# Column groups of a projection taken in pairs, seven products of halves instead of eight

## The chip, the cores and the metric

The kernel runs on one core of one Trainium2 chip. The metric is the device time of one execution in microseconds (us); lower is better. A core has TensorE (matrix products into PSUM), VectorE, ScalarE and GpSimd (element-wise work; GpSimd reads no PSUM here), and SyncE, whose queue starts most DMAs. In the profile's rows they are PE (PEld for its weight loads), DVE, ACT, POOL and SP.

## The reference

Two layers of a hybrid block on `x` of 512 rows by 1024 columns, all float32. In each layer:

```
h = rmsnorm(x, norm_g)
u = h @ w_in                      # 1024 x 9312; columns split into named parts
ml:  q, k by a causal convolution of 4 taps and silu; mLSTM over 4 heads of 256 with gates i, f
     y_ml  = rmsnorm(mlstm * sigmoid(o)) * silu(z)
gla: gated linear attention, 4 heads (64 / 128), decay from a rank-16 projection
     y_gla = rmsnorm(gla) * silu(r)
dsa: scores of 8 small index heads choose 128 keys a query (top-k); attention over these, 4 heads
     y_dsa = dsa * silu(z)
x = x + concat(y_ml, y_gla, y_dsa) @ w_out     # 2048 x 1024
```

The projection `h @ w_in` and the product with `w_out` are most of the arithmetic.

## The kernel before

**Matmuls.** Each float32 operand is cut into a high and a low float32r part, and a product is three matmuls, high by high, high by low and low by high (`mm3`, line 509). `xhi` and `xlo` (405, 406) hold the two parts of the normed input, transposed: 8 blocks of 128 along the 1024 inputs (KT) by 512 rows.

**Column groups.** The columns of `w_in` are worked off in groups of 256, in the order of `group_order` (66): values of the GLA, a small group `misc`, index queries, GLA queries and keys, then PLAN (105): three ML heads (o, q, k, v), a closing, the fourth head, a closing, two DSA units, two closings. In the plain form (`proj_n`, 524; PSUM tile `pn`) the input is the stationary operand and 256 columns of weights are streamed: 4 row blocks by 8 k-blocks by 3 matmuls, 96 a group. In the transposed form (`proj_t`, 514; PSUM tile `pt`) the weights are stationary and the 512 rows are streamed: 2 column blocks by 8 by 3, 48 a group. A closing (`y_group`, 724, and `w_out_part`, 733) projects two gate groups, multiplies them into a branch's output (`y_part`, 693), and multiplies 512 columns of the result with their part of `w_out` in 8 chunks (PSUM tile `pw`), each added into the residual `xr`, which stays in SBUF (385).

**Weights.** They come from DRAM in halves of a group, 128x1024, on SP's queue (`load`, 449). ScalarE writes the high part, VectorE the low part (`split_part`, 467), a few halves ahead of use.

**Order.** The schedule is written out when the program is built. Between the matmuls of a group, `tick` (505) issues a part of the weight splitting and then stages of background tasks: recurrences, convolutions, attention, top-k. Whether a task's next stage is issued is read from a clock kept with estimated durations (`Clock`, 207; `Background.due`, 304): not before what it reads should be there, and not while ScalarE, VectorE or GpSimd would be more than 11 us behind. On the chip each engine takes its instructions in that fixed order and waits on semaphores. At the start of a layer the norm of a row block (`norm_in`, 625) squares, scales, transposes and splits it.

**PSUM.** Three banks rotate among projections (`pp`, 360), five among the background tasks (`pa`, 365).

Of the kernel before, what the change touches and what calls it, by code (L numbers as in the profile page):

```python
# [20 lines left out]
S = 512  # L21
D = 1024
# [42 lines left out]

def group_order():
    order = []

    def cols(name, g=0):
        order.append(("in", OFF[name] + 256 * g))  # L70

    def out(q):
        order.append(("out", 512 * q, 0))
        order.append(("out", 512 * q, 512))

    def unit(kind, g):
        if kind == "dsa":
            for n in ("dsa_q", "dsa_k", "dsa_v"):
                cols(n, g)
        else:  # L80
            for n in ML_ORDER:
                cols(n, g)

    def steps(plan):
        for step in plan:
            if step[0] == "close":
                for g in range(2):
                    cols(step[1], step[2] + g)
                out(step[3])
            else:  # L90
                unit(*step)

    cols("gla_v", 0)
    cols("gla_v", 1)
    order.append(("misc",))
    cols("idx_q", 0)
    cols("idx_q", 1)
    order.append(("gqk", 0))
    order.append(("gqk", 1))
    steps(PLAN)  # L100
    return order


ML_ORDER = ("ml_o", "ml_q", "ml_k", "ml_v")
PLAN = (("ml", 0), ("ml", 1), ("ml", 2), ("close", "ml_z", 0, 0), ("ml", 3), ("close", "gla_r", 0, 2), ("dsa", 0), ("dsa", 1), ("close", "ml_z", 2, 1), ("close", "dsa_z", 0, 3))


def pack_weights(w_in, w_out):
    order = group_order()
# [28 lines left out]
BEHIND = {"sel": ("dve",)}  # L138
BACKLOG = {None: 11.0, "sel": 0.3}
ALONE = ("gla", "ml", "sel", "scores")  # L140
BUFFERS = {"gla": 6, "dsa": 2, "ml": 4, "mlv": 1, "conv": 2, "qk": 2, "y": 2, "scores": 4, "gates": 5}
# [24 lines left out]
class Meter:  # L166
    """Passes instructions on to an engine and books them on the engine's estimated clock (us)."""
# [15 lines left out]
    def cost(self, op, args, kw):  # L183
# [3 lines left out]
        if self.name == "pe":  # L187
            if op == "transpose":
                return 0.109
            n, one_pass = free_size(out), kw["rhs"].dtype == F32R  # L190
            if one_pass:
                return max(n, 256) / 2400 + 0.002
            if out.shape[0] == 64:
                return max(n / 950, 0.08)
            return max(4 * n, 256) / 2400 + 0.004
# [11 lines left out]
class Clock:  # L207
    """Estimated time at which each engine gets done with what it has been given; an operation starts when
    its engine is free and what it reads has been written."""
# [12 lines left out]
    def ring(self, tag, tile, bufs):  # L222
        """The tile takes the place of the one made bufs tiles before it."""
        ring = self.rings.setdefault(tag, [])
        ring.append(tile.name)
        if len(ring) > bufs:
            old = ring.pop(0)
# [38 lines left out]
class Background:  # L266
    """Tasks cut into stages: a stage is issued once what the stage before it made should be there."""
# [36 lines left out]
    def due(self, task):  # L304
        late = BACKLOG.get(task["kind"], BACKLOG[None])
        return max(task["ready"], max(self.clock.at[e] for e in BEHIND.get(task["kind"], ("act", "dve", "pool"))) - late)
# [26 lines left out]
def hybrid_kernel(ctx, tc, a, out, dbg=None):  # L333
# [15 lines left out]
    N_T4, N_T2, N_F8, VA_BUFS = 9, 19, 2, 1  # L349
    W_BUFS, LOAD = 5, 4.5  # L350
# [19 lines left out]
    def t4(name, n=1024):  # L370
        return wk.tile([128, 1024], F32, tag="t4", name=name, bufs=N_T4)[:, 0:n]
# [3 lines left out]

    def f8(name):
        return wk.tile([128, 2048], F32R, tag="f8", name=name, bufs=N_F8)
# [7 lines left out]
    xr = const.tile([128, NB, D], F32, name="xr")  # L385

    def load_x(sb):
        nc.sync.dma_start(xr[:, sb, :], a["x"][0, 128 * sb:128 * sb + 128, :])

    load_x(0)  # L390
# [15 lines left out]
    xlo = const.tile([128, KT, S], F32R, name="xlo")  # L406
    qzs = [const.tile([128, 2, 64 * NB], F32, name=f"qz{i}") for i in range(2)]
# [5 lines left out]
    # (scale * mean + scale * eps) ** -0.5  # L413
# [4 lines left out]
    # two float32r parts of a value in PSUM, with a gain per partition and block: high first, low a stage later  # L418
# [23 lines left out]
    # one tag holds what was loaded and the low parts; a slot of it stays free while halves wait to be split  # L442
    order = [(layer, i) + spec for layer in range(DEPTH) for i, spec in enumerate(group_order())]
    halves_of = [1 if spec[2] == "misc" else 2 for spec in order]
    to_load = [(k, half) for k in range(len(order)) for half in range(halves_of[k])]
    loaded, ready, parts, half_done = {}, {}, [], []
    state = {"held": 0, "split": 0, "used": 0, "done": 0}

    def load(limit):
        while to_load and state["held"] < limit:  # L450
            state["held"] += 1
            k, half = to_load.pop(0)
            layer, i = order[k][:2]
            raw = wp.tile([128, 1024], F32, tag="w", name=f"raw{k}_{half}", bufs=W_BUFS)
# [3 lines left out]
    def split():  # L458
        k = state["split"]
        if k == len(order):  # L460
            return
# [43 lines left out]
    def tick():  # L505
        split_part()
        bg.tick()
# [848 lines left out]
```

## Time and profile before

| | |
|---|---|
| time, median of 3 runs | 1238.54 us (1236.86 to 1240.45) |
| profiled execution: its span, first to last instruction | 1236.4 us |
| what lies between that span and the median | 2.1 us |
| TensorE busy | 1215.7 us, 8308 matmuls |
| VectorE, ScalarE, GpSimd busy | 830.5, 583.2, 162.0 us |
| granted TensorE clock | 9 tenths or more in every slice |
| DMA | 107.98 MB, mean 87 GB/s |

The page gives no total for the profiled execution beyond its span; the span is its own time here, and the median of the runs stands beside it. Busy TensorE time is the union of matmuls whose ends are modelled, so that consecutive ones overlap in the rows; the distance between two starts is what one takes. Idle time of an engine that nothing waits for costs nothing.

### The profile page before, as it was taken

To read this page: it belongs to the slowest core of one execution; us is meant where nothing else is said; L and a number is where in the kernel's file an instruction comes from. 1 tells how busy PE (TensorE), PEld (TensorE's weight loads), DVE (VectorE), ACT (ScalarE), POOL (GpSimd) and SP (SyncE) were. 2 spreads that over 40 slices of the span, in tenths; PEclk is the share of its full clock that TensorE was granted. 3 is DMA by queue.
4 is the path that set the end of the run, shared out by engine and by line. 5 is a ranking of instruction groups with operands and counts; after the bars stand their busy time and mean duration, and the time that the engine had idled before them with its cause. 6 is when DMAs were issued, how large, how long until landed. Compare 5 with 4: busy or idle time off the path is not lost.

```text
span 1236.4 us, 20867 instructions
## 1 busy us (share of the span) xinstructions
PE 1215.7 (98%) x8308; PEld 1095.3 (89%) x8308; DVE 830.5 (67%) x1618; ACT 583.2 (47%) x1214; POOL 162.0 (13%) x293
## 2 busy tenths in 40 slices
PE   6999999999999999999999999999999999999998
PEld 6978889899889898998898889898988998989997
DVE  5479869796887844364556978888888875234643
ACT  6564546444153265542357544564442443554321
POOL 2003112300000013200010121031210000122000
PEclk9999999999999999999999999999999999999999
DMA  4333222222222223323223223122222322313222
GB/s 160 107 108 100 87 69 78 69 78 69 83 97 96 76 71 109 112 69 102 69 70 120 69 71 106 57 93 77 69 67 71 111 69 92 123 52 116 67 83 102
DMA packets 35169, 107.98 MB, mean 87 GB/s; under 512 B 5028, under 2 KB 8388, under 8 KB 35072
## 3 DMA queue, kind: packets, MB, share of 16 engines
q1 hardware_dynamic: 33136, 104.89, 26.0%
q8 instruction: 65, 1.06, 0.4%
q0 software_dynamic: 1200, 1.36, 0.3%
q10 hardware_dynamic: 736, 0.41, 0.1%
q14 instruction: 32, 0.26, 0.1%
HBM read 104.48 MB, written 3.43 MB: 87 GB/s over the span
## 4 chain that ended last, share of the span: by engine, by line
PE 93%; DVE 2%; ACT 2%; DMA 1%; POOL 1%; issue 1%; SPq 0%; DVEq 0%; POOLq 0%
PE pn L180 42%; PE pt L180 22%; PE pw L180 14%; PE psS L180 2%; PE pom L180 2%; PE pod L180 2%; PE psga L180 1%; PE pss L180 1%; PE pog L180 1%; PE psy L180 1%; DMA bs<-skew 1%; POOL bs L180 1%; PE psl L180 1%; DVE lo L180 1%; ACT xhi L180 1%
## 5 line engine op out<-in xcount | busy, mean ns | idle before, releaser
L180 PE MATMUL pn<-hi,xhi 128*128 128x256 f32 x1536 | 445.2, 290 | 0.0
L180 PE MATMUL pn<-hi,xlo 128*128 128x256 f32 x1536 | 434.4, 283 | 1.0 <-DVE xlo L180 1.0
L180 PE MATMUL pn<-lo,xhi 128*128 128x256 f32 x1536 | 433.6, 282 | 1.3 <-DVE lo L180 1.3
L180 DVE TENSOR_TENSOR lo<-raw,hi 128x1024 fp32r<-128x1024 f32 x178 | 221.9, 1247 | 184.4 <-ACT hi L180 178.1
L180 PEld LDWEIGHTS pn<-lo,xhi 128*128 128x128 f32 x1536 | 291.6, 190 | 4.0 <-DVE lo L180 1.7
L180 PEld LDWEIGHTS pn<-hi,xhi 128*128 128x128 f32 x1536 | 289.9, 189 | 4.4 <-PE psl L180 1.0
L180 PEld LDWEIGHTS pn<-hi,xlo 128*128 128x128 f32 x1536 | 290.3, 189 | 1.5 <-DVE xlo L180 1.5
L180 ACT ACTIVATE hi<-raw 128x1024 fp32r<-128x1024 f32 x178 | 188.1, 1057 | 117.2 <-DMA raw<-w_pack 89.4
L180 PE MATMUL pt<-xhi,hi 128*128 128x512 f32 (+1 forms) x400 | 158.8, 397 | 0.0
L180 PE MATMUL pt<-xlo,hi 128*128 128x512 f32 (+1 forms) x400 | 154.5, 386 | 0.0
L180 PE MATMUL pt<-xhi,lo 128*128 128x512 f32 (+1 forms) x400 | 154.5, 386 | 0.0
L180 PE MATMUL pw<-hi,yhi 128*128 128x512 f32 x256 | 102.2, 399 | 0.0
L180 PE MATMUL pw<-hi,ylo 128*128 128x512 f32 x256 | 101.6, 397 | 0.0
L180 PE MATMUL pw<-lo,yhi 128*128 128x512 f32 x256 | 101.4, 396 | 0.0
L180 PEld LDWEIGHTS pt<-xhi,hi 128*128 128x128 f32 x400 | 75.2, 188 | 17.6 <-issue 4.2
L180 PEld LDWEIGHTS pt<-xhi,lo 128*128 128x128 f32 x400 | 75.3, 188 | 15.3
L180 PEld LDWEIGHTS pt<-xlo,hi 128*128 128x128 f32 x400 | 75.4, 189 | 12.6
L180 DVE TENSOR_TENSOR xr<-pw,xr 128x512 f32<-128x512 f32 x64 | 44.1, 689 | 51.0 <-PE pw L180 50.9
L180 DVE SCALAR_TENSOR_TENSOR cacc<-cbuf,pv,cacc 128x512 f32<-128x512 f32 x96 | 74.5, 776 | 2.5 <-ACT cacc L180 0.2
L180 ACT ACTIVATE th<-pn 128x512 f32<-128x512 f32 x32 | 19.2, 599 | 86.7 <-PE pn L180 86.7
L180 PEld LDWEIGHTS pw<-hi,ylo 128*128 128x128 f32 x256 | 48.2, 188 | 12.6 <-DVE ylo L180 1.2
L180 ACT ACTIVATE cbuf<-pt 128x512 f32<-128x512 f32 x32 | 19.1, 597 | 84.0 <-PE pt L180 79.7
(187 smaller groups left out, 1694.9 us busy)
## 6 DMA issues: line engine op xcount, KB each, us to landing
raw<-w_pack SPq DMA_DIRECT2D x178, 512.0 KB, 3.9
xr<-x SPq DMA_DIRECT2D x4, 512.0 KB, 7.7
negm<-negm SPq DMA_DIRECT2D x8, 256.0 KB, 5.2
bs<-skew SPq DMA_DIRECT2D x8, 256.0 KB, 6.1
out_dram<-xr SPq DMA_DIRECT2D x8, 256.0 KB, 2.0
bs<-skew SPq DMA_DIRECT2D x8, 192.0 KB, 6.3
skew<-flat POOLq DMA_DIRECT2D x1, 1280.0 KB, 17.9
bs<-skew SPq DMA_DIRECT2D x8, 128.0 KB, 5.5
```

The costliest lines, as they stand in the source:

```text
L180: return f(*args, **kw)
```

## The change

Two column groups are projected together. The 512 rows of the input, the 1024 inputs and the two groups are each halved, so that the product is a 2 x 2 by 2 x 2 product of blocks: eight products of 256 rows by 512 inputs by 256 columns. It is computed as seven (Strassen, in Winograd's arrangement), of sums of input quadrants and sums of weight halves. Three of the sums of the input (`xsum`) are formed once a layer and split again in two parts; a fourth takes the place of the quadrant (rows 256 to 511, inputs 0 to 511) in `xhi` and `xlo` once the groups that use it plainly are done. The weight sums are formed on GpSimd for each pair, four additions of 128x1024. In each layer 15 pairs go this way: two for each ML head (q with k in the transposed form, o with v), three for DSA (q with k, v with v, q with k), four at the closings. The GLA values, `misc`, index queries, and GLA queries and keys stay as they were, and so does `w_out`.

Beside it: high parts, low parts, loaded halves and sums share one tag of 15 buffers; low parts go to GpSimd or VectorE, whichever the clock has free first; all large tiles share one tag of 12; the residual lives in DRAM, to which the closings but the last of a layer add with accumulating DMAs of GpSimd's queue, and the last one reads it back; chunks of `w_out` run over the row blocks in the order 2, 3, 0, 1; the transposed form streams 256 rows at a time; the DMA scratch is 2048 bytes and the copy of the bias goes in two halves.

```diff
-    N_T4, N_T2, N_F8, VA_BUFS = 9, 19, 2, 1
-    W_BUFS, LOAD = 5, 4.5
+    N_T4, N_T2 = 12, 16
+    W_BUFS, LOAD = 15, 4.5
...
-    xr = const.tile([128, NB, D], F32, name="xr")
+    resid = dram.tile([S, D], F32, name="resid", bufs=1)
...
+    xsum = [[const.tile([128, 4, 256], F32R, name=f"x{n}{part}") for part in "hl"] for n in "567"]
...
+                b11, b12, b22, b21 = (Raw((layer, at + g, half)) for g, half in ((0, 0), (1, 0), (1, 1), (0, 1)))
+                s1 = Raw(sources=(b11, b12))
...
+                s2 = Raw(sources=(s1, b22))
+                s4 = Raw(sources=(s2, b21))
+                room += [b11, b12, s1, b22, ("add", b12, b22), s2, b21, s4]
+                pieces_of.append([Piece(b11, n, -1.0)] + [Piece(r, n) for r in (b12, s2, b21, s1, s4, b22)])
...
+            nc.gpsimd.tensor_tensor(dst.tile, ins[0].tile, ins[1].tile, op=OP.add)
...
+            engine = nc.gpsimd if clock.at["pool"] + POOL_LOW < clock.at["dve"] else nc.vector
+            engine.tensor_tensor(lo, p.raw.tile, hi.bitcast(F32), op=OP.subtract)
...
+    def prepare():
+        make_room()
+        said = [add_up(), split_low(), split_high()]
+        return said
...
     def tick():
-        split_part()
+        prepare()
         bg.tick()
...
+    def pair(form, f, dest=lambda c, r: None):
+        pieces = list(next_unit(7))
+
+        def product(x, ps, first=False):
+            wh, wl = need(pieces.pop(0))
+            for blk in range(2):
+                o = ps[:, 256 * blk:256 * blk + 256]
+                s = slice(128 * blk, 128 * blk + 128)
+                for kb in range(4):
+                    xs = [t[:, kb, :] for t in x]
+                    if form == "n":
+                        ops = xs[0][:, s], xs[1][:, s], wh[kb], wl[kb]
+                    else:
+                        ops = wh[kb][:, s], wl[kb][:, s], xs[0], xs[1]
+                    mm3(o, *ops, first and blk == 0 and kb == 0, kb == 3, skip_group_check=True)
+                if blk == 0:
+                    tick()
+            give_back(1)
+
+        def copied(ps):
+            t = t2("snap")
+            nc.scalar.activation(t, ps, AF.Copy)
+            return t
+
+        def result(c, r, ps, t=None):
+            d = dest(c, r)
+            if t is not None:
+                d = t if d is None else d
+                nc.vector.tensor_sub(d, like(ps, d), like(t, d))
+            elif d is not None:
+                nc.scalar.activation(d, like(ps, d), AF.Copy)
+            f(c, r, ps if d is None else d)
...
+        x5, x6, x7 = xsum
+        pa1, pc = pp("pr1"), pp("pr7")
+        product(quad(0, 0), pa1, True)
+        p1 = copied(pa1)
+        tick()
+        product(x7, pc, True)
+        p7 = copied(pc)
+        tick()
+        product(x6, pa1)
+        u2 = copied(pa1)
+        tick()
+        pb = pp("pr2")
+        product(quad(0, 1), pb, True)
+        result(0, 0, pb, p1)
...
+        product(x5, pa1)
+        result(1, 1, pa1, p7)
...
+        product(quad(1, 1), pc)
+        result(0, 1, pc, u2)
...
+        product(quad(1, 0), pa1)
+        result(1, 0, pa1)
+        tick()
...
-                dst = xr[:, sb, 512 * half:512 * half + 512]
-                nc.vector.tensor_tensor(dst, ps, dst, op=OP.add)
+                if after:
+                    dst = rows[sb][:, c]
+                    nc.vector.tensor_tensor(dst, ps, dst, op=OP.add)
+                    if after == "store":
+                        nc.sync.dma_start(out[0, s, c], dst)
+                    elif half:
+                        nc.sync.dma_start(resid[s, :], rows[sb])
+                        norms[sb] = norm_task(layer + 1, sb)
+                else:
+                    t = t2("wo")
+                    nc.scalar.activation(t, ps, AF.Copy)
+                    nc.gpsimd.dma_start(resid[s, c], t, accum_op=OP.add)
...
-                for sb in range(NB):
+                for n, sb in enumerate((2, 3, 0, 1)):
...
+            if last:
+                for sb in range(NB):
+                    load_rows(sb, resid)
```

## Rows read from the trace of the kernel before

**Rows 1.** The page, part 1: engine, busy us (share of the span), instructions.
```profile
PE 1215.7 (98%) x8308; PEld 1095.3 (89%) x8308; DVE 830.5 (67%) x1618; ACT 583.2 (47%) x1214; POOL 162.0 (13%) x293
```

**Rows 2.** The page, part 4: the chain of waits, shares by line.
```profile
PE pn L180 42%; PE pt L180 22%; PE pw L180 14%; PE psS L180 2%; PE pom L180 2%; PE pod L180 2%; PE psga L180 1%; PE pss L180 1%; PE pog L180 1%; PE psy L180 1%; DMA bs<-skew 1%; POOL bs L180 1%; PE psl L180 1%; DVE lo L180 1%; ACT xhi L180 1%
```

**Rows 3.** TensorE's waits, whole span: us in total, times, longest us.
```profile
PE psx L180 <- ACT xs L180: 9.5, 1, 9.5
...
PE pn L180 <- DVE lo L180: 1.3, 2, 0.7
```

**Rows 4.** Timeline of TensorE, plain form: start us, us, instruction; 29 consecutive matmuls.
```profile
139.43 0.28 PE L180 MATMUL pn<-lo,xhi 128*128 128x256 f32 x1
...
142.79 0.28 PE L180 MATMUL pn<-hi,xlo 128*128 128x256 f32 x1
```

**Rows 5.** Timeline of TensorE, transposed form: 11 consecutive matmuls.
```profile
121.74 0.39 PE L180 MATMUL pt<-xlo,hi 128*128 128x512 f32 x1
...
124.08 0.39 PE L180 MATMUL pt<-xhi,lo 128*128 128x512 f32 x1
```

**Rows 6.** Groups by line, whole span: busy us, mean ns | idle before, releaser.
```profile
L180 ACT ACTIVATE hi<-raw 128x1024 fp32r<-128x1024 f32 x178 | 188.1, 1057 | 117.2 <-DMA raw<-w_pack 89.4 <-PE pw L180 25.3 <-DVE xr L180 2.1
L180 DVE TENSOR_TENSOR xr<-pw,xr 128x512 f32<-128x512 f32 x64 | 44.1, 689 | 51.0 <-PE pw L180 50.9
L180 ACT ACTIVATE th<-pn 128x512 f32<-128x512 f32 x32 | 19.2, 599 | 86.7 <-PE pn L180 86.7
L180 DVE TENSOR_TENSOR val<-pn,vah 128x512 fp32r<-128x512 f32 x16 | 11.0, 688 | 0.2
```

**Rows 7.** Timeline of GpSimd and of VectorE, 195 to 200.
```profile
195.03 1.04 POOL L180 TENSOR_TENSOR za<-ta 128x512 f32<-128x512 f32 x1 [15.05 <-DVE dn L180]
196.03 2.09 POOL L180 TENSOR_TENSOR dec<-ta 128x256 f32<-128x256 f32 x2
196.54 3.15 DVE L180 SCALAR_TENSOR_TENSOR cacc<-cbuf,pv,cacc 128x512 f32<-128x512 f32 x3
```

**Rows 8.** The same operations where they do not meet: timelines near 116 and 134.
```profile
115.96 1.25 POOL L180 TENSOR_TENSOR dec<-ta 128x256 f32<-128x256 f32 x2
133.69 2.32 DVE L180 SCALAR_TENSOR_TENSOR cacc<-cbuf,pv,cacc 128x512 f32<-128x512 f32 x3
```

**Rows 9.** Groups by line of GpSimd: an issue of a DMA.
```profile
L180 POOL DMA_DIRECT2D li<-misc x2 | 1.4, 708 | 27.9 <-ACT misc L180 27.9
```

**Rows 10.** Stretches: length, busy us of PE, PEld, DVE, ACT, POOL; PEclk, DMA, GB/s.
```profile
50.00:300.00 250.00, 249.89 (x1726) 218.82 (x1725) 201.85 (x348) 136.28 (x262) 45.30 (x81) 1.00 0.26 83
650.00:900.00 250.00, 249.16 (x1696) 219.19 (x1695) 204.37 (x350) 135.24 (x243) 41.59 (x79) 1.00 0.25 81
```

**Rows 11.** Groups by line of VectorE, 50 to 300, its two largest.
```profile
L180 DVE TENSOR_TENSOR lo<-raw,hi 128x1024 fp32r<-128x1024 f32 x36 | 44.3, 1232 | 20.4 <-ACT hi L180 14.6 <-ACT gq L180 5.5
L180 DVE SCALAR_TENSOR_TENSOR cacc<-cbuf,pv,cacc 128x512 f32<-128x512 f32 x36 | 28.9, 802 | 1.0 <-ACT cacc L180 0.2
```

**Rows 12.** Timeline of VectorE at the layer boundary: one row block.
```profile
618.59 0.69 DVE L180 TENSOR_TENSOR xr<-pw,xr 128x512 f32<-128x512 f32 x1 [0.98 <-PE pw L180]
...
626.75 1.13 DVE L180 SCALAR_TENSOR_TENSOR xlo<-psx,pv,xhi 128x128 fp32r<-128x128 f32 x4
```

**Rows 13.** The chain of waits in order of time, last closing of layer one.
```profile
597.53 0.61 ACT th L180
...
600.29 19.67 PE pw L180 x84
```

**Rows 14.** DMA issues: KB each, median us to landing.
```profile
xr<-x SPq DMA_DIRECT2D x4, 512.0 KB, 7.7
```

More of the change, by code (lines that the diff above doesn't have):

```diff
@@ L84, in steps @@
[L84 to L100, printed above, removed]
-    return order
-ML_ORDER = ("ml_o", "ml_q", "ml_k", "ml_v")
@@ L439, in split_task @@
             low_part(ps, hi, lo)
[L443 to L454, printed above, removed]
-            nc.sync.dma_start(raw, a["w_pack"][layer, i, :, 1024 * half:1024 * half + 1024])
-            loaded[k, half] = (raw, clock.at["pe"] + LOAD)
@@ new lines, in w_tile, with read, make_room @@
+    def w_tile(name, dtype):
+        return wp.tile([128, 1024], dtype, tag="w", name=name, bufs=W_BUFS)
+    def read(raw):
+        raw.readers -= 1
+        if not raw.readers:
+            state["used"] -= 1
+    def make_room(limit=W_BUFS - 3):
+        while room and (isinstance(room[0], tuple) or state["used"] < limit):
+            r = room.pop(0)
+            if isinstance(r, tuple):
+                sums.append(r)
+                continue
+            state["used"] += 1
+            if r.src is None:
+                sums.append(r)
+            else:
+                layer, i, half = r.src
+                r.tile = w_tile("raw", F32)
+                nc.sync.dma_start(r.tile, a["w_pack"][layer, i, :, 1024 * half:1024 * half + 1024])
+                r.ready = clock.at["pe"] + LOAD
@@ new lines, in due_at, with add_up @@
+    def due_at(raw):
+        return raw.ready if raw.ready is not None and raw.whole else None
+    def add_up():
+        if not sums:
+            return None
+        head = sums[0]
+        ins = head[1:] if isinstance(head, tuple) else head.sources
+        if any(r.ready is None for r in ins):
+            return None
+        late = max(r.ready for r in ins)
+        if late > clock.at["pe"]:
+            return late
+        sums.pop(0)
+        if isinstance(head, tuple):
+            dst, other = ins
+            nc.gpsimd.tensor_tensor(dst.tile, dst.tile, other.tile, op=OP.add)
+            dst.whole = True
+            read(other)
+        else:
+            dst = head
+            dst.tile = w_tile("sum", F32)
+            nc.gpsimd.tensor_tensor(dst.tile, ins[0].tile, ins[1].tile, op=OP.add)
+            for r in ins:
+                read(r)
+        dst.ready = clock.at["pool"] + SEMAPHORE
+        return True
@@ new lines, in prepare, with need, next_unit @@
+    def prepare():
+        make_room()
+        said = [add_up(), split_low(), split_high()]
+        return said
+    def need(piece):
+        while piece.parts is None:
+            said = prepare()
+            if True not in said:
+                late = [t for t in said if t is not None]
+                assert late, "no room for weights"
+                clock.at["pe"] = max(clock.at["pe"], min(late))
+        state["held"].append(piece)
+        return piece.parts
+    def next_unit(n):
+        k = state["unit"]
+        assert len(pieces_of[k]) == n or n < 3 and len(pieces_of[k]) < 3
+        state["unit"] += 1
+        return pieces_of[k]
```

460 lines of the change are left out of this document (259 added, 201 removed).

## The prediction

> **What bounds the kernel now.** I read the page's busy shares first: TensorE 98%, VectorE 67%, ScalarE 47%, GpSimd 13% [rows 1]. A busy TensorE proves little, because the ends of matmuls are modelled. So I looked next at the chain of waits, with 42% of the span in `pn`, 22% in `pt` and 14% in `pw` [rows 2], and then at TensorE's own waits: the worst is a single one of 9.5 us at the start [rows 3]. The engine never starves, so the time is the number of columns that it streams. What one matmul costs is the distance between starts, not the 0.28 us or 0.40 us shown as its length. From 139.43 to 142.79 there are 28 steps of `pn`, 0.120 us each for 256 columns [rows 4]. From 121.74 to 124.08 there are 10 steps of `pt`, 0.234 us each for 512 [rows 5]. Halving the width from 512 to 256 is therefore nearly free: 0.240 us for two halves.
>
> **What leaves TensorE.** A pair of column groups takes 8 products of halves now and 7 after. A product is 2 blocks by 4 k-blocks by 3 matmuls, so 24 matmuls of 256 columns. Each layer has 15 pairs: eight of the four ML units, three of DSA, four at the closings. Four of them (q with k) are in the transposed form. For the 22 pairs in the plain form, 24 x 0.120 = 2.88 us each goes, 63.4 us in all. For the 8 transposed pairs, 96 x 0.234 = 22.5 us becomes 168 x 0.120 = 20.2 us, 18.4 us in all. Together that is -81.8 us, all of it on the path that sets the end, as long as TensorE remains the engine that others wait for.
>
> **What is added beside it, engine by engine.**
>
> Weights split: 178 halves now, 58 + 30 x 7 = 268 after. The 90 more cost ScalarE 1.06 us each (95 us). With 90 snapshots of PSUM at the 0.60 us of an ACT copy (54 us) and 48 copies of `wo` (29 us), less the 32 copies of `cbuf` (19 us), ScalarE goes from 583 to about 742 us of 1155 [rows 1, 6]: 64%, hidden under TensorE. If it weren't, its copies are the ones that let an accumulator be reused (below).
>
> GpSimd gets four sums of 128x1024 a pair, 120 in all, and 8 a layer for the input. No such sum is in the trace. From 256 columns (0.61 us when alone: two in 1.25) to 512 (1.04) it grows by 0.43 us [rows 7, 8], so 1024 takes 1.04 + 0.86 = 1.9 us by that slope, and 2.5 us if four times the 256. I take 1.9: 136 x 1.9 = 258 us. Then there are the low parts that it takes over from VectorE. The code gives one to whichever of the two it believes to be free first; I assume half, 134 x 1.9 = 255 us. With 48 DMA issues at 0.7 us [rows 9] GpSimd goes from 162 to about 710 us, 61%.
>
> VectorE: 134 low parts instead of 178 (-54 us), 90 subtractions out of PSUM at 0.69 us, the time of `val` (+62), 48 fewer residual additions (-33) [rows 6]. From 831 it goes to some 806 us, 70% of the shorter span. On busy time alone, all three side engines still fit.
>
> **Where they don't fit.** GpSimd and VectorE take turns when both read two operands in SBUF. From 196.03 on, GpSimd's subtractions take 2.09 us for two, against 1.25 for two alone; the VectorE operations beside them take 3.15 us for three, against 2.32 alone [rows 7, 8]. A GpSimd step and a VectorE step run at one per 1.04 us, where alone they add up to 0.62 + 0.77 = 1.39: a pair of such steps takes 75% of their sum. Operations out of PSUM seem spared: `xr` and `val`, 512 columns with one operand in PSUM, have means of 0.69 us [rows 6], that of such an operation left alone. The Trainium skill says the same and more strictly (SBUF — State Buffer, "Who interferes with whom"): a VectorE instruction with two SBUF inputs and a GpSimd instruction that reads SBUF exclude each other, and the loser blocks for the whole instruction. The rows agree on the turns, and show a quarter of the sum still overlapping. By that rule alone, with nothing overlapping, the kernel ends where the second rival below does.
>
> Now the two stretches in which this matters, 50 to 300 and its like at 650 to 900. VectorE is busy 202 and 204 of 250 us there, against 831 - 406 = 425 us in the other 736 [rows 1, 10]. Three ML units lie in one, so 6 pairs: TensorE's 250 us become 250 - 6 x 2.73 = 234. GpSimd must then fit 24 + 8 sums and half of 54 low parts, 59 x 1.9 = 112 us, and what it does already, about 25 us without stretching. VectorE's two-input operations are the larger form of `cacc` 29, its 27 low parts 33, and about 75 in groups of under 13 us each (`qz`, the other `cacc`, `dec`, `acc`, the low parts of q and k), 137 us [rows 11]. The sum is 274 us in 234. At 75% it is 206, 88% of the stretch. It fits on paper, but the order is fixed in advance by a clock that prices no such turn, and the queues are in order: behind a VectorE operation that waits for its turn stand the subtractions that free PSUM and the low parts that TensorE needs. The loss lies between 0 (206 fits) and 274 - 234 = 40 us a stretch. I take 18 us, a little under the middle, because the row nearest to it shows the overlap; 36 us for both. In the rest of each layer VectorE has slack, and I charge nothing.
>
> **Ends and corners.** At the layer boundary the row blocks now finish in the order 2, 3, 0, 1, but the next layer begins with block 0. From the residual addition of a block at 618.59 to its last `xlo` at 627.88 takes 9.3 us [rows 12]; the one chunk left to cover it is 12 x 0.234 = 2.8 us. That is 6.5 us of idle TensorE, once (before, the covering chunks were three). At a closing, from the last evacuation to `w_out` the chain is tanh, two VectorE steps and the transposes, 597.53 to 600.29 [rows 13], then a high and a low part, some 4.1 us and 0.7 more for the new subtraction; the last product covers 2.9. Six of the eight closings have background work for the other 2 us; the last of each layer hasn't: 4 us. Between 0 and 16 for all eight. Residual accumulation in DRAM: 48 DMAs on GpSimd's queue, each waiting for its `wo` copy, with sums and low parts queued behind. I cost it at nothing since weights are prepared ahead. A landing took up to 7.7 us (512 KB of `x`) [rows 14]; if each had to await the one before it, 8 x 7.7 = 62 us would be needed per `w_out` of 8 x 12 x 0.234 = 22.5 us, about 40 too late. The rows of the residual move through SP's queue: four loads ahead of the last closing of a layer, four stores at the boundary, each of the size of a weight half, 512 KB. They stand in front of the weight loads, whose landings they delay by about one load's time each; 15 buffers hide that, and the doubled copy of the bias and the copy of `x` to DRAM on GpSimd's queue fall in the first 50 us, before a sum is due. Both at nothing; without that cover a load late by 7.7 us at each boundary, 15 us.
>
> **Sum.** 1236.4 - 81.8 + 36 + 6.5 + 4 = 1201 us of span. The profiled span is 2.1 us under the median of 1238.5, so the forecast is 1203 us.
>
> **Rivals.**
>
> *TensorE keeps its cover.* Turns cost nothing: 1203 - 36 = 1167 us. For it: no wait of TensorE on a low part above 0.7 us now [rows 3], at 81% load in those stretches. Against it: [rows 7].
>
> *Turns decide, slower.* VectorE and GpSimd become the bound in both stretches. With nothing overlapping, +40 each: 1167 + 80 = 1247 us. With all low parts on GpSimd, 27 x (1.9 - 1.23) = 18 more each: 1283. It is slower once a stretch loses over 36 us, so when turns save under a tenth of the sum. For it: 274 us of demand in 234. Against it: the 75%.
>
> *A shorter leash on PSUM.* Now three accumulators rotate at one per 5.7 us. After, an accumulator must be copied or subtracted while one other product runs, 24 x 0.120 = 2.9 us. Wherever ScalarE or VectorE lags more, TensorE waits. One us at two handovers a pair, 60 us instead of the 36: 1227 us. For it: tasks may be issued until an engine is 11 us behind by the kernel's own clock. Against it: copies out of PSUM almost always wait for TensorE now, for instance `th` for 86.7 us [rows 6].
>
> *The DRAM residual holds GpSimd up*, so that the pairs behind it start late, 40 us at two of the six places after the others are covered: 1167 + 2 x 40 = 1247 us. Against it: the eight chunks write different rows, and the next `w_out` comes tens of us later.
>
> **Chances.** Forecast (1180 to 1222) 0.42; cover kept 0.20; PSUM leash 0.10; turns decide 0.22; DRAM residual 0.06. Within 0.3% (3.7 us) of before is about what a measurement of this kernel can't tell from no change. Of the leash and the DRAM case a little falls there or above. Faster 0.69, same 0.06, slower 0.25. The range is 1163 to 1262 us; the likeliest case alone is 1180 to 1222.
>
> **What would show it.** Right: 8308 - 528 + 576 = 8356 matmuls, those of the products 0.120 us apart, `pn` and `pt` replaced by the seven products; low parts on VectorE lengthening from 1.23 to 1.6 us or more in the mean; TensorE's waits on low parts and on PSUM handovers of 30 to 60 us in total, mostly in the first 45% of each layer; a gap of some 6 us at the boundary. Wrong: TensorE's waits under 20 us (cover kept), or VectorE near 100% over those stretches (turns decide), waits that name ScalarE's snapshots (leash), or GpSimd idle before accumulating DMAs (residual). A clock of TensorE under the 1.00 of [rows 10] after such waits would add to them.

## The result and the profile after

The changed kernel takes 1509.89 us (median; 1508.17 to 1515.4) against 1238.04 for the kernel before: a ratio of 1.2196, with a 95% interval of 1.2168 to 1.2223. I had forecast 1203 us, a gain of 35; it is a loss of 272. The profiled execution spans 1513.7 us.

The page, part 1, busy us, to set beside [rows 1]:

```profile
PE 1238.5 (82%) x8356; PEld 1129.9 (75%) x8356; DVE 1140.9 (75%) x1628; ACT 732.3 (48%) x1408; POOL 921.4 (61%) x593
```

The matmuls are the 8356 that I counted, and ScalarE is within 10 us of my sum. VectorE is 335 us above it, GpSimd 211. TensorE's waits, whole span (us in total, times, longest us), beside [rows 3]:

```profile
PE psga L174 <- DVE qz L174: 81.6, 19, 8.3
PE pr L174 <- DVE snap L174: 23.6, 5, 9.6
PE pskd L174 <- DVE za L174: 20.6, 4, 6.8
PE pr L174 <- DVE lo L174: 17.3, 7, 5.8
PE psy L174 <- DVE dsa_v L174: 14.5, 5, 6.4
PE psx L174 <- ACT xs L174: 14.0, 3, 9.1
PE pr L174 <- ACT snap L174: 11.6, 7, 2.3
...
PE pw L174 <- DVE ylo L174: 8.1, 4, 2.6
```

Most name VectorE, and the first names `qz`, a small product of the tasks beside the projections, not a low part. The stretches with most of the ML groups (columns as in [rows 10]):

```profile
150.00:400.00 250.00, 186.19 (x1412) 177.67 (x1410) 224.76 (x260) 119.04 (x209) 165.87 (x109) 0.85 0.18 60
900.00:1150.00 250.00, 180.04 (x1423) 172.77 (x1422) 234.78 (x297) 116.34 (x201) 161.39 (x105) 0.86 0.18 61
```

VectorE has 225 and 235 of 250 us and TensorE 180 to 186: the sign that I had given for "turns decide". TensorE's granted clock averages 0.85 and 0.86 there, 1.00 in [rows 10], so the waits are paid a second time. Over the whole span it is at the lower of its two levels (1.2 GHz) in 45 stretches of together 288 us, before in two of together 5; matmuls of 256 columns that start there are 0.213 us apart instead of 0.119. I sorted the distances between the starts of consecutive matmuls into three: what a matmul of its shape takes at full clock (the 20th percentile of the shape), the excess of those that start at the lower clock, up to one more such step, and the rest, mostly waits. That gives 1118, 1 and 104 us before; 1036, 78 and 386 after. The products save 82 us, as forecast; the lower clock costs 77 and the waits 282.

What happens in one such gap: timelines of VectorE, GpSimd and TensorE (start us, us, instruction [idle before <- releaser]):

```profile
211.01 0.83 DVE L174 TENSOR_TENSOR dec<-dec,gk 128x256 f32<-128x256 f32 x1
211.76 5.04 DVE L174 TENSOR_TENSOR qz<-dec,gq 64x256 f32<-64x256 f32 x2
...
211.57 2.47 POOL L174 TENSOR_TENSOR raw<-raw 128x1024 f32<-128x1024 f32 x1
214.00 2.51 POOL L174 TENSOR_TENSOR sum<-sum,raw 128x1024 f32<-128x1024 f32 x1
...
216.95 1.12 PE L174 MATMUL psga<-qz,dec 128*64 128x64 f32 x16 [6.31 <-DVE qz L174]
```

Two `qz`, 0.45 us each where nothing disturbs them (below), take 5.04 us and end 0.3 us after GpSimd's second sum. The sums keep nearly the length that they have alone (2.34 to 2.40 us); TensorE stands for 6.31 us, and during this wait its clock falls. The groups by line show the same in the mean (busy us, mean ns | idle before):

```profile
L174 POOL TENSOR_TENSOR lo<-raw,hi 128x1024 fp32r<-128x1024 f32 x89 | 229.2, 2576 | 137.7 <-ACT hi L174 101.5 <-DVE qz L174 8.1 <-DVE lo L174 7.9
L174 POOL TENSOR_TENSOR sum<-sum,raw 128x1024 f32<-128x1024 f32 x60 | 160.3, 2671 | 5.8 <-PE pt L174 3.3 <-DVE lo L174 2.1 <-POOL lo L174 0.2
...
L174 DVE TENSOR_TENSOR lo<-raw,hi 128x1024 fp32r<-128x1024 f32 x59 | 113.0, 1916 | 114.6 <-ACT hi L174 95.9
L174 DVE SCALAR_TENSOR_TENSOR cacc<-cbuf,pv,cacc 128x512 f32<-128x512 f32 x96 | 135.1, 1419 | 3.4 <-issue 1.0
L174 DVE TENSOR_TENSOR qz<-dec,gq 64x256 f32<-64x256 f32 x56 | 51.4, 919 | 0.4
L174 DVE TENSOR_TENSOR snap<-pr,snap 128x512 f32<-128x512 f32 x60 | 40.9, 685 | 22.6 <-PE pr L174 19.1 <-issue 3.1
L174 DVE TENSOR_TENSOR val<-snap,vah 128x512 fp32r<-128x512 f32 x8 | 15.7, 1956 | 0.0
L174 DVE TENSOR_TENSOR val<-pr,vah 128x512 fp32r<-128x512 f32 x8 | 5.4, 681 | 0.0
```

The last two rows are one and the same subtraction. Read out of PSUM it takes 0.68 us; where the change has moved its operand to a tile in SBUF it takes 1.96. `snap<-pr`, with an operand in PSUM, is as short as such operations were. Over all groups, VectorE's operations with two operands in SBUF are 310 us longer than at their undisturbed length (the 5th percentile of each group; 19 us before), all others 23 (11 before).

### The profile page after: what moved, and what is told of

It reads as the page before. It is cut to its first block, busy times and chain, and to the rows that moved or that the text cites. A ratio compares the mean times of both kernels' runs of the same rounds, so it can differ in the third digit from the quotient of the medians.

```text
span 1513.7 us, 21848 instructions
## 1 busy us (share of the span) xinstructions
PE 1238.5 (82%) x8356; PEld 1129.9 (75%) x8356; DVE 1140.9 (75%) x1628; ACT 732.3 (48%) x1408; POOL 921.4 (61%) x593
## 5 line engine op out<-in xcount | busy, mean ns | idle before, releaser
L174 POOL TENSOR_TENSOR lo<-raw,hi 128x1024 fp32r<-128x1024 f32 x89 | 229.2, 2576 | 137.7 <-ACT hi L174 101.5
L174 PE MATMUL pr<-hi,xhi 128*128 128x256 f32 x704 | 208.1, 296 | 23.6 <-DVE snap L174 23.6
L174 PE MATMUL pr<-lo,xhi 128*128 128x256 f32 x704 | 203.6, 289 | 1.4 <-DVE lo L174 0.9
L174 PE MATMUL pr<-hi,xlo 128*128 128x256 f32 x704 | 203.1, 288 | 0.0
L174 DVE TENSOR_TENSOR lo<-raw,hi 128x1024 fp32r<-128x1024 f32 x59 | 113.0, 1916 | 114.6 <-ACT hi L174 95.9
L174 POOL TENSOR_TENSOR sum<-sum,raw 128x1024 f32<-128x1024 f32 x60 | 160.3, 2671 | 5.8 <-PE pt L174 3.3
L174 PEld LDWEIGHTS pr<-hi,xhi 128*128 128x128 f32 x704 | 138.4, 197 | 25.6 <-DVE snap L174 20.0
L174 PEld LDWEIGHTS pr<-lo,xhi 128*128 128x128 f32 x704 | 138.5, 197 | 2.8 <-DVE lo L174 1.1
L174 POOL TENSOR_TENSOR lo<-sum,hi 128x1024 fp32r<-128x1024 f32 x41 | 110.6, 2700 | 45.6 <-ACT hi L174 42.9
L174 PEld LDWEIGHTS pr<-hi,xlo 128*128 128x128 f32 x704 | 138.0, 196 | 0.0
L174 POOL DMA_DIRECT2D resid<-wo x48 | 44.1, 959 | 127.8 <-ACT wo L174 111.7
L174 PEld LDWEIGHTS psga<-qz,dec 128*64 128x64 f32 x416 | 22.1, 176 | 86.8 <-issue 32.8
```

Source lines behind the costliest of these rows:

```text
L174: return f(*args, **kw)
```

## The experiments

Theories for the first four: *turns* (GpSimd's two-operand reads of 128x1024 block VectorE), against *GpSimd is late* and *a shorter leash on PSUM*. Each "before" beside them lies between 1237.7 and 1240.0 us.

**The weight sums without reads.**
```diff
-            nc.gpsimd.tensor_tensor(dst.tile, dst.tile, other.tile, op=OP.add)
+            clock.book("pool", 0.1 + 1024 / 560, [dst.tile], [dst.tile, other.tile])
+            for c in range(2):
+                bass_nc.gpsimd.memset(dst.tile, 0.01)
```
The other sum likewise.

> Each weight sum of the changed kernel (120 of them) is left out and replaced on GpSimd by two plain fills of the same 128x1024 tile, about 2.1 us together beside the 2.4 us of the sum; the order of all other work is the same instruction for instruction. GpSimd so stays about as busy and the tiles are about as late, but it reads no SBUF for them. Theory of turns (VectorE operations with two SBUF operands wait while GpSimd reads): GpSimd's reading operations of weights fall from 250 to 130, so the 310 us by which VectorE's two-operand operations are stretched fall to about 160, and the time from 1510 to 1330 to 1400 us. Rival, GpSimd is simply late with what TensorE needs: GpSimd's time falls by 0.3 us a sum, under 40 us in all, and the time stays above 1470 us. Rival, short leash on PSUM, or accumulating DMAs: no change, 1490 to 1515 us.

1386.74 us (ratio 1.1182, 1.1149 to 1.1214), inside the range for turns: 123 us go, with the order of instructions unchanged. VectorE's two-operand instructions now exceed their undisturbed length by 196 us instead of 310. GpSimd isn't quite as busy as I had expected, since two fills take 1.96 us where a sum took 2.66:

```profile
PE 1206.7 (87%) x8356; PEld 1106.3 (80%) x8356; DVE 1008.6 (73%) x1628; ACT 730.9 (53%) x1408; POOL 826.0 (60%) x713
```

So this run alone leaves room for lateness; the next one doesn't.

**All low parts on VectorE.**
```diff
-            engine = nc.gpsimd if clock.at["pool"] + POOL_LOW < clock.at["dve"] else nc.vector
+            engine = nc.vector
```

> All 268 low parts on VectorE, none on GpSimd; the weight sums stay on GpSimd. VectorE gets 130 x 1.23 = 160 us of its own work more, GpSimd loses 130 x 2.6 = 340 us. Theory of turns: the stretch of VectorE's two-operand operations falls by about half, 310 to 150 us, which the added work eats up: VectorE's busy time stays near 1140 us and the time falls only a little, 1430 to 1500 us. Rival, GpSimd late: freed of 340 of its 921 us, it delivers the sums early, and the time falls to 1300 us or less. Rival, PSUM leash: more load on VectorE, 1510 us or more.

1491.72 us (1.2028, 1.1994 to 1.2063), inside the range for turns. VectorE takes 130 instructions more and the kernel is still 18 us shorter. GpSimd has 339 us less to do, and if it had merely been late the time would have fallen to 1300 us or less:

```profile
PE 1225.0 (82%) x8356; PEld 1121.5 (75%) x8356; DVE 1143.4 (77%) x1758; ACT 727.9 (49%) x1408; POOL 582.0 (39%) x463
```

**Both edits:** GpSimd reads no weights.

> Weight sums left out (filled on GpSimd for as long, as above) and all low parts on VectorE: GpSimd reads no weights at all, VectorE carries its full own load of about 1141 - 310 + 160 = 990 us. Theory of turns: VectorE's two-operand operations are back at their own lengths (1.23 us a low part, 0.75 us cacc), and the time is 1180 to 1230 us, the forecast without the turns plus some lag of a VectorE 80% busy. Rival, PSUM leash or accumulating DMAs: what they cost stays, and the time stays at 1350 us or above. Rival, GpSimd late with sums: the fills still take 2.1 us, so 1400 us or above.

1356.63 us (1.0939, 1.0907 to 1.0971): 153 us less than the changed kernel, and 127 more than the upper end expected. Page, part 1, and two groups:

```profile
PE 1192.1 (88%) x8356; PEld 1094.0 (81%) x8356; DVE 983.6 (73%) x1758; ACT 727.1 (54%) x1408; POOL 487.3 (36%) x583
...
L174 DVE SCALAR_TENSOR_TENSOR cacc<-cbuf,pv,cacc 128x512 f32<-128x512 f32 x96 | 72.8, 768 | 2.8 <-ACT cacc L174 0.5
...
L174 DVE TENSOR_TENSOR qz<-dec,gq 64x256 f32<-64x256 f32 x56 | 24.9, 445 | 0.4
```

`cacc` and `qz` are back at 0.77 and 0.45 us: the turns are gone, but not the loss. TensorE's longest wait, with what the other queues held (GpSimd, VectorE, ScalarE, TensorE):

```profile
888.27 1.24 POOL L174 TENSOR_TENSOR za<-ta 128x512 f32<-128x512 f32 x1 [11.66 <-DVE ta L174]
891.50 1.96 POOL L514 MEMSET raw<- 128x1024 f32 x2
...
885.41 0.68 DVE L174 MATCH_REPLACE8 acc<-m,acc 128x512 f32<-128x512 f32 x1
886.72 1.37 DVE L174 TENSOR_TENSOR_SCAN ta<-za 128x128 f32<-128x128 f32 x4
...
893.49 1.06 ACT L174 ACTIVATE hi<-raw 128x1024 fp32r<-128x1024 f32 x1 [0.60 <-POOL raw L514]
...
894.60 0.58 PE L174 MATMUL pr<-hi,x7h 128*128 128x256 f32 x1 [13.72 <-ACT hi L174]
```

Read it upwards: TensorE waits for a high part, that for a fill on GpSimd, the fill stands behind `za`, `za` waits for the scan `ta`, and the scan stands on VectorE behind the search for the largest scores (`MATCH_REPLACE8`). Queues in order carry VectorE's lateness to engines that have time.

**Sums and low parts on VectorE,** nothing left out (`nc.vector` in the three places).

> Nothing is left out: weight sums and low parts both on VectorE. VectorE's own load is 990 + 120 x 1.23 = 1140 us, GpSimd keeps only its old work and the sums of the input. Theory of turns: no stretch but a VectorE near 95% of a TensorE-bound span, in the stretches of the ML units well above 100%, so 1250 to 1350 us: faster than the changed kernel although VectorE has more work, slower than before. Rival, PSUM leash: with so full a VectorE the subtractions come later still, 1500 us or more.

1392.64 us (1.1229, 1.1197 to 1.1262). VectorE does all of GpSimd's work on weights as well, and the kernel is 117 us faster:

```profile
PE 1200.3 (86%) x8356; PEld 1094.3 (79%) x8356; DVE 1123.0 (81%) x1878; ACT 726.8 (52%) x1408; POOL 289.6 (21%) x343
```

So turns hold. But the time is 43 us above the range, and the version of 1356.63 us, without turns on weights, still lies some 190 us over the 1167 of the forecast without turns. The theories for these 190 us are L (VectorE's load by itself), W (too short a lead of weight tiles), B (too few small tiles), later D (the structure around the products).

**Half of each low part** (512 columns, read twice), on the version of 1356.63:
```diff
-        lo = w_tile("lo", F32R)
+        lo = w_tile("lo", F32R)[:, 0:512]
...
-            engine.tensor_tensor(lo, p.raw.tile, hi.bitcast(F32), op=OP.subtract)
+            engine.tensor_tensor(lo, raw, part, op=OP.subtract)
```

> Left out: half of every low part of a weight (the low product reads the other half twice). It starts from the version that took 1356.63 us, in which GpSimd reads no weights; TensorE's matmuls, the tiles and the order written out stay, only VectorE's 268 low parts go over 512 columns instead of 1024, about 268 x 0.55 = 147 us less on VectorE, which brings it from 984 us to about 835, what it has before the change. Theory L (what remains over 1167 us is VectorE: in the stretches of the ML groups it has 40 to 47 of every 50 us to do, and what TensorE waits for stands behind that): 1200 to 1250. Theory W (the lead is short: a product of halves uses up a weight tile in 24 x 0.120 = 2.9 us where a plain group takes 5.8, and the same few tiles lie ahead, so each hold-up of an engine's queue reaches TensorE): 1310 to 1345, since only the subtraction itself gets shorter. Theory B (13 instead of 19 small tiles are left for the tasks beside the projections, so fewer of them run at once): 1330 or more.

1271.2 us (1.0267, 1.0249 to 1.0285). VectorE falls by 144 us to 840, the time by 85: most of what theory L asked for, though 21 us above its range, and far under those of W and B.

**21 weight tiles,** in the room of the activation sums:
```diff
-    W_BUFS, LOAD = 15, 4.5
+    W_BUFS, LOAD = 21, 4.5
...
-        x5, x6, x7 = xsum
+        x5, x6, x7 = quad(0, 0), quad(0, 1), quad(1, 1)
```

> Left out: beside the weight sums, the sums of the activations (the products read quarters of the activations as they are, so the three sum tiles are not needed). The 24 KB per partition so freed give 21 weight tiles instead of 15. It starts from the version that took 1356.63 us. Theory W (short lead of weight tiles): six more tiles are two more pieces split ahead, 2 x 2.9 = 5.8 us more lead against waits that are mostly 2 to 8 us long: 1240 to 1300. Theory L (VectorE's load) and theory B (small tiles): 1325 or more, the missing sums of the activations giving some 10 to 20 us at the most around the start of each layer.

1304.35 us (1.0527, 1.051 to 1.0545), 4 us above the range of theory W. But two things changed here; the control below separates them.

**True prices in the planner:**
```diff
-            return 0.07 + n / 960 + 0.06 * min(pointers, 1)
+            return 0.13 + n / 915 + 0.06 * min(pointers, 1)
```

> Starts from the version that took 1356.63 us and changes only the prices with which the order of the instructions is worked out: VectorE 0.13 + n/915 us instead of 0.07 + n/960, ScalarE 0.13 + n/1110 instead of 0.11 + n/1250, GpSimd 0.08 + n/441 instead of 0.1 + n/560, matmuls 256/2180 instead of 256/2210, all as read from the traces (a subtraction over 1024 columns 1.22 us, a copy 1.05, a sum 2.40, a step 0.120). Theory O, a part of theory L (the written order believes VectorE to be some 10 per cent quicker than it is; where VectorE is nearly full it falls behind this plan, and matmuls of the units are put into TensorE's queue before their operands can be there, so that TensorE stands at their head): 1260 to 1320. Theory L without it (VectorE simply has too much to do): 1335 to 1370. Theories W and B: 1335 to 1380.

1348.4 us (1.0881, 1.0857 to 1.0905): 8 us, the range of theory L without O. Prices that are some 10 per cent off are not the matter.

**The kernel before with 13 small tiles** (`N_T2` 19 to 13).

> The kernel before the change with one size changed: 13 small tiles instead of 19 for the tasks beside the projections, what the changed kernel leaves them while a pair of groups is worked on. Theory B (the tasks beside the projections lack tiles): 1300 or more, a good part of the 190 us that are open. Theories L and W: within 25 us of the kernel before, 1238 to 1265.

1324.47 us (1.069, 1.0673 to 1.0707): 86 us dearer, with TensorE's longest waits on `za` (29.5 us) and `qz` (22.1), which stand high in the changed kernel too.

**Control: without the activation sums, 15 and 16 tiles.**

> Left out: the weight sums and the sums of the activations; nothing else differs from the version that took 1356.63 us (15 weight tiles, 16 small tiles). It shows what the missing sums of the activations alone are worth, which the version with 21 weight tiles and the next one have in common: 1335 to 1357 by all theories, since these sums are some 16 GpSimd instructions and 6 splits in a layer. If it comes out near 1304, the 21 weight tiles were worth nothing and theory W (short lead of weight tiles) falls.

1317.27 us (1.0633, 1.0617 to 1.0649), under all that I expected. The activation sums cost 39 us and the six weight tiles are worth only 13. The page, part 1, and the start of the layers (stretches, as in [rows 10]; with the sums, then without):

```profile
PE 1185.2 (90%) x8356; PEld 1086.9 (83%) x8356; DVE 971.1 (74%) x1750; ACT 718.7 (55%) x1400; POOL 449.7 (34%) x567
```

```profile
40.00:110.00 70.00, 62.04 (x298) 50.03 (x297) 51.05 (x69) 37.21 (x59) 26.34 (x24) 0.95 0.35 120
690.00:790.00 100.00, 89.44 (x514) 77.17 (x512) 74.61 (x129) 61.09 (x116) 38.61 (x34) 0.96 0.25 84
```

```profile
40.00:110.00 70.00, 70.00 (x380) 58.11 (x379) 50.84 (x76) 45.64 (x75) 17.68 (x23) 1.00 0.38 127
690.00:790.00 100.00, 99.89 (x637) 88.17 (x637) 78.23 (x113) 61.27 (x97) 25.09 (x31) 1.00 0.25 81
```

TensorE loses 18 us there; the other 21 lie elsewhere. VectorE's two-operand instructions exceed their undisturbed length equally in both (31 us), so these 39 us aren't turns; what they are was not taken further apart.

**22 small tiles** in that room instead (`N_T2` 16 to 22).

> Left out: the weight sums and the sums of the activations. Of the room that the latter free, 12 KB per partition go to small tiles: 22 instead of 16, so that 18 are left to the other tasks while three hold what a pair of groups has set aside, as many as the kernel before has. Theory B (too few small tiles; 13 instead of 19 cost the kernel before 86 us): 50 to 90 us less than the version without these sums, 1250 to 1295. If VectorE's load alone decided here: within 15 us of that version.

1321.39 us (1.0655, 1.0618 to 1.0693): nothing, as the other theory said. Theory B holds for the kernel before, and falls for this version of the changed one.

**Half low parts, 22 small tiles, 17 weight tiles.**

> Left out: the weight sums, the sums of the activations, and half of every low part of a weight. With 22 small tiles and 17 weight tiles. If VectorE's load (85 us by the run with half low parts), the small tiles (50 to 90) and the lead of the weight tiles (a third of 52 with two more tiles) together are what was open over 1167 us, 1356.63 less these is 1150 to 1215, below the kernel before. If something else holds this structure back (the residual in DRAM, the order of the products, the PSUM tiles of a pair), it stays at 1230 or more.

1233.25 us (0.9958, 0.9944 to 0.9972): 84 us under the control, which is what the half low parts gave before. Tiles add nothing again, and the time is in the range that speaks for something else in the structure.

```profile
PE 1160.4 (94%) x8356; PEld 1066.8 (87%) x8356; DVE 821.9 (67%) x1750; ACT 717.3 (58%) x1400; POOL 426.7 (35%) x567
```

**All on VectorE, 21 small and 12 weight tiles,** nothing left out.

> Computes everything. The version with sums and low parts on VectorE (1392.64 us), with 21 small tiles in place of 16 and 12 weight tiles in place of 15, which is what fits into the same room. Theory B over W: the small tiles give 50 to 85 us, the three weight tiles cost 10 to 40: 1320 to 1380. If the lead of the weight tiles is worth more than the small tiles: 1395 or more. In no theory does it come below the kernel before, since VectorE keeps some 120 x 1.25 = 150 us of sums and 90 x 1.22 = 110 us of further low parts.

1398.15 us (1.1297, 1.1273 to 1.1321), against 1392.64: no gain. Both counts change at once here, so these 5 us don't say what each is worth.

**VectorE's load put on the kernel before:**
```diff
-            nc.vector.tensor_sub(lo, raw, hi.bitcast(F32))
+            for _ in range(2 if state["split"] % 3 else 1):
+                nc.vector.tensor_sub(lo, raw, hi.bitcast(F32))
```

> The kernel before, with two of every three groups of weights having their low parts subtracted a second time into the same tiles: some 119 more instructions of 128x1024 on VectorE, 119 x 1.25 = 149 us, which brings VectorE from 831 us to about 980, what it has in the changed kernel without turns on weights. TensorE, tiles and the rest stay. Theory L (VectorE's load, by itself, makes TensorE wait once VectorE has 45 of every 50 us to do beside the ML groups): 1295 to 1330. If a load of that size is absorbed by the old schedule and only the new one suffers: 1265 or less.

1292.79 us (1.0431, 1.0414 to 1.0448), 2 us under the range of theory L. VectorE goes from 831 to 975 us, the time 53 us up: 0.37 us for each us, on an engine that is 76% busy over the span and 85 and 82% in the stretches of [rows 10]:

```profile
PE 1234.2 (96%) x8308; PEld 1105.6 (86%) x8308; DVE 974.8 (76%) x1738; ACT 585.9 (45%) x1214; POOL 181.1 (14%) x293
```

**Low parts of 64 columns,** on the version of 1233.25.

> Left out: the weight sums, the sums of the activations, and the low parts of the weights but for 64 columns of each (the low products read the high parts). It starts from the version of 1233.25 us and takes another 268 x about 0.55 = 147 us from VectorE, and TensorE no longer waits for a low part. Theory L (VectorE's load is also the rest of what is open over 1167 us): 1170 to 1205. Theory D (the rest is the structure: transposed outputs, the closings, the layer boundary with the residual in DRAM, the order of seven products): 1215 or more.

1205.34 us (0.9738, 0.9708 to 0.9768), at the edge of what L allowed: another 121 us off VectorE, and no low part that TensorE waits for, give only 28.

```profile
PE 1147.6 (95%) x8356; PEld 1058.6 (88%) x8356; DVE 701.0 (58%) x1750; ACT 717.8 (60%) x1400; POOL 418.7 (35%) x567
...
PE pw L174 <- DVE ylo L174: 17.1, 7, 3.5
PE psx L174 <- ACT xs L174: 14.2, 2, 9.2
PE psy L174 <- DVE dsa_v L174: 8.6, 3, 4.3
```

What is left are the closings (`pw`, `psy`) and the layers' starts (`psx`).

**Without the accumulating DMAs.**
```diff
-                    nc.gpsimd.dma_start(resid[s, c], t, accum_op=OP.add)
```

> Left out: as in the version of 1233.25 us, and the 48 accumulating DMAs into the residual, so the later layers read a residual that lacks them. If these, or what GpSimd waits for ahead of them, hold the kernel up (theory D's DRAM part): 1215 or less. If they lie beside other work, as I had put them at 0: 1225 to 1240.

1230.67 us (0.993, 0.9915 to 0.9944): 3 us. In this version, in which GpSimd reads no weights, my zero for the accumulation in DRAM stands. In the changed kernel, where GpSimd has 921 us to do and waits 111.7 us for `wo`, it wasn't tried.

**Seven products for 12 pairs only,** nothing left out: the 18 pairs up to the last ML unit of each layer by eight products of halves, two of them accumulated in PSUM; sums and low parts on VectorE.
```diff
+PLAIN = 9
...
+            elif pairs < PLAIN:
+                pairs += 1
+                raws = [Raw((layer, at + g, half)) for g, half in ((0, 0), (0, 1), (1, 0), (1, 1))]
+                room += raws
+                pieces_of.append([Piece(r, n) for r in raws])
...
+        if len(pieces_of[state["unit"]]) == 4:
+            return plain_pair(form, f, dest)
```

> Computes everything. Seven products only for the 12 pairs that follow the ML groups of a layer, where VectorE has 20 to 30 of every 50 us to do; the other 18 pairs by eight products of halves, accumulated in PSUM; weight sums and low parts on VectorE. TensorE loses 12 x 24 x 0.120 = 34.6 us. VectorE gains 48 sums x 1.25 + 36 low parts x 1.22 + 24 differences x 0.69 = 121 us, where it has room. If VectorE's load in the ML stretches is what the change died of: 1205 to 1245. If the smaller tile counts or the new structure cost as much there as well: 1260 to 1320.

1287.22 us (1.038, 1.036 to 1.04), 42 us above the range for VectorE's load in the ML stretches and inside that for costs of the structure or of tiles. (Each pair takes three differences, not the two I counted.)

```profile
PE 1213.4 (94%) x8788; PEld 1115.6 (87%) x8788; DVE 955.8 (74%) x1698; ACT 665.0 (52%) x1324; POOL 274.8 (21%) x343
```

**The same with eight products for all 30 pairs** (`PLAIN = 15`, no activation sums).

> Computes everything. The changed kernel's structure (pairs of groups by quarters of the output, residual in DRAM, 16 small tiles and 12 large ones, 15 weight tiles) with eight products for all 30 pairs, so without weight sums, sums of the activations, 90 of the low parts and 60 differences. VectorE is back at about 830 us and TensorE has the matmuls of before. If seven products alone bring the loss (VectorE's load, turns): 1232 to 1250, as the kernel before. If the structure around them costs by itself (fewer tiles for the tasks beside, quarters done only at the end of a pair, the closings): 1262 to 1310.

1268.85 us (1.0252, 1.023 to 1.0274). The structure around the products costs 31 us by itself. Page, part 1, and the largest waits of TensorE:

```profile
PE 1223.0 (96%) x9076; PEld 1137.5 (90%) x9076; DVE 806.0 (64%) x1570; ACT 613.2 (48%) x1262; POOL 217.1 (17%) x327
...
PE psx L175 <- ACT xs L175: 15.3, 2, 8.9
PE psy L175 <- DVE so L175: 6.1, 4, 3.0
...
PE pw L175 <- DVE ylo L175: 1.1, 1, 1.1
```

**And with 22 small and 14 large tiles.**

> The version with eight products for all pairs, with the 24 KB per partition of the three activation sums, which it does not use, given to tiles: 22 small ones instead of 16 and 14 large ones instead of 12. If the tile counts are what the structure costs (13 small tiles cost the kernel before 86 us): 25 to 60 us less than the version with 16 and 12, down to 1238. If not: within 10 us of it, and the rest belongs to the order of quarters and to the closings.

1268.41 us (1.0248, 1.0231 to 1.0264): the counts of small and large tiles are not at fault.

The step from this version to the one with 12 seven-product pairs is +18 us where TensorE does 35 less. VectorE does 150 more (806 to 956), and 150 x 0.37, the price from the loaded kernel before, is 55; 55 - 35 = 20. By this estimate a VectorE that is busy for 30 of 50 us was not room. It isn't shown alone, since the activation sums and the dearer closings come with seven products too.

## Why the prediction was wrong, step by step

The ledger, each step a difference of two runs but for the saving of TensorE, which is worked out: 1238 before; +31 the structure with eight products (1269); -86 for 30 products of 24 x 0.120; +22 not taken apart, with 17.1 us on `ylo` at closings that waited 1.1 with eight products; that is 1205, without weight sums, activation sums and nearly all low parts. Then +28 and +84 for the low parts on VectorE (1233, 1317), +39 for the activation sums (1357), and +153 for GpSimd's reads of weights (1510), net of the 130 low parts that VectorE takes over without them.

**TensorE's -81.8 us:** right (82 by the starts).

**ScalarE hidden:** right (732 us for 742; its snapshots cost TensorE 11.6 us).

**The turns, 18 us a stretch, 36 in all: this is the step that failed.** Without GpSimd's reads of weights the kernel is 153 us faster, and 117 with all that work on VectorE. First the size of a sum: I took 1.9 us by the slope from 256 to 512 columns, but neither row of that slope, `dec` or `za`, adds two full tiles: one operand is spread out from single columns (lines 933 and 955). Alone a sum takes 2.34 to 2.40, four times the 0.61 of [rows 8], and beside VectorE 2.66 to 2.67 in the mean (`lo` 2.58 and 2.70). Then the rule: in [rows 7] both engines had steps of similar length, and I read off a quarter of overlap. GpSimd's steps on weights are 3 to 5 times as long as VectorE's `cacc` and `qz`, and VectorE's short step waits for nearly all of one: above, each `qz` ends 0.3 us after a sum of 2.5 us. The Trainium skill's stricter rule (SBUF — State Buffer, "Who interferes with whom"), by which the loser blocks for the whole instruction, agrees with these rows. The rival in which nothing overlaps named the right mechanism. But its 1247 to 1283 was far too low as well, since I capped its loss at demand minus supply in two stretches. The delay is paid by chains: `qz` waits, the matmuls written behind it wait, and TensorE's clock falls, which alone costs 77 us in the changed kernel. Third, the change itself made more such operations: its snapshots moved operands of `val` and of the gates' products from PSUM to SBUF. I had written that operations out of PSUM are spared, and didn't ask which of them would no longer be out of PSUM. My sign for being right, low parts of 1.6 us or more, came true (1.92), but TensorE's largest wait was on `qz`, not on low parts or PSUM handovers.

**"On busy time alone, all three side engines still fit", and nothing charged outside the stretches:** wrong, and worth 84 us without any turn, the step from 822 us on VectorE, about what it has before the change, to 971. The sum of VectorE's time may fit, but in a queue in order each of its instructions delays those behind it, as the rows at 888 us show. I priced its work at zero below 100%, and it costs 0.37 us per us from 67 to 76% (the kernel before), 0.56 between 822 and 971 us (84 / 149), 0.23 between 701 and 822. The split of the low parts that I assumed (134 on GpSimd) was 130.

**The boundary, 6.5 us:** right. TensorE's second wait for `xs` is 15.3 - 8.9 = 6.4 us with eight products. **The closings, 4 us:** too low. TensorE's waits on `psy` and `pw` add up to 1.1 us before, 13.9 with eight products and 31 in the version of 1205 us. With the boundary and some 5 us for the narrower steps that is some 24 of the 31 us of the structure. The activation sums, which I counted only as GpSimd time, cost 39.

**The PSUM leash** as a rival: 11.6 + 23.6 us of waits on snapshots in the changed kernel, 3.2 + 4.5 in the version of 1356.63 us, so mostly a result of the turns. **The residual in DRAM:** 3 us where it was tried, not the 80 of the rival; the 7.7 us of [rows 14], which I called a most, is a median. **SP's moves at nothing:** no run speaks against it, and none tries it.

No version here that computes everything beats the kernel before.

## What to carry to other kernels

A product saved on the bound engine has to be set against what its bookkeeping costs on the engines beside it, at their price and not at zero. Here a pair saves TensorE 2.88 us and gives VectorE 4 sums x 1.25 + 3 low parts x 1.22 + 3 differences x 0.69 = 10.7 us; at 0.37 that is 4.0, by this estimate a loss even where turns don't occur. To learn the price, put dummy work of that size on the kernel before: one run, and its price would have spoken against this change. And look for operands that a change moves from PSUM to SBUF, and for long GpSimd instructions set beside short VectorE ones.

## What the runs showed of the hardware

GpSimd's addition of two 128x1024 float32 tiles takes 2.34 to 2.40 us alone; a fill of the same tile takes 0.98 and left VectorE's two-operand instructions nearly alone (31 us of excess in the version of 1356.63 us, where the reads gave 310). VectorE loses most by those turns: a 0.75 us `cacc` took up to 2.9 us, while GpSimd's sums grew by about 0.3 in the mean. VectorE's instructions of 512 columns with an operand in PSUM kept their 0.68 us beside it. At the lower of TensorE's two clock levels matmuls of 256 columns were 0.213 us apart, at the full one 0.119.
